# Routing of a product-key expert layer: key numbers on bf16, the slot as the inner index, the best scores copied by ScalarE

## The chip, the cores and the metric

The kernel runs on one core of a Trainium2 chip. The metric is the time of one execution on the device in microseconds, the median over runs. A second source is the profile: one execution as the hardware profiler recorded it, with every instruction of every engine.

The engines are TensorE (PE, its weight loads PEld), VectorE (DVE), ScalarE (ACT), GpSimd (POOL) and SyncE (SP, which here only issues DMAs). Each works through its own queue in program order.

## The reference

The network has two mLSTM blocks with their feed-forward layers and one block with attention, which ends in an expert layer (PEER) and a final norm, on 256 tokens of width 1024. The change lies in the expert layer:

```python
def block(xb):                                              # 128 tokens
    q = (xb @ w_q).reshape(n, PEER_HEADS, 2, PEER_HALF)     # 8 heads, 2 halves
    s = jnp.einsum('nhpc,hpkc->nhpk', q, sub_keys)          # 128 keys per half
    s_top, i_top = lax.top_k(s, PEER_TOPK)                  # the best 16 of each half
    cand_s = (s_top[:, :, 0, :, None] + s_top[:, :, 1, None, :]).reshape(n, PEER_HEADS, -1)
    cand_i = (i_top[:, :, 0, :, None] * N_KEYS + i_top[:, :, 1, None, :]).reshape(n, PEER_HEADS, -1)
    best_s, best_pos = lax.top_k(cand_s, PEER_TOPK)         # the best 16 of 256 pairs
    ids = jnp.take_along_axis(cand_i, best_pos, axis=-1)
    gate = jax.nn.softmax(best_s, axis=-1)
    act = gelu(jnp.einsum('nd,nhkd->nhk', xb, u[ids]))
    return jnp.einsum('nhk,nhkd->nd', (gate * act), v[ids])
```

## The kernel before, in words

The kernel doesn't gather experts. It computes the hidden value of all 16384 experts for all 256 tokens (128 "units" of 128 experts each, weights `pu`), multiplies them by a dense weight that is zero for experts not chosen, and multiplies by `pv`. The dense weights come out of the routing by one-hot products on TensorE.

Every weight tile streams through one helper: a DMA brings `wraw`, ScalarE rounds it to `whi` (L113), and the remainder `wlo` (L119) is a subtract on the engine `ws.sub`. In the stretch of interest `ws.sub` is GpSimd; `weights()` sets it to VectorE when it begins. Four tiles of `whi` and three of `wlo` are held, so a new one starts when a unit of TensorE is finished. A unit is 24 matmuls (L279 to L281), whose result ScalarE passes through Gelu into `store` (L228). Two banks hold results, so unit j + 2 needs the Gelu of unit j.

The last stretch has this order in the program. First sixteen query units with their key scores. Then a loop over the first 72 of the 128 units (`STORE`). After each unit the loop calls `bg(UBUD)` with `UBUD` 2.6, which hands background work to the queues: it adds 2.6 to a credit, and while the credit is above zero it draws one step from the first generator in the list and takes the number that the step yields off the credit. So the yields of a generator decide behind which unit each of its steps stands in the queues of all engines. The list holds the last `keys` generators (top 16 of the scores), then `route(0)`, `route(1)` and `weights()`.

`route(t)`, for 128 tokens, is nearly all VectorE: the key numbers as float (`fi`, L1627), the 256 sums of each head (`cand`, L1631), eight steps of top 16 (L1612 to L1616, values into `best`, places into `pos`), place to pair of slots by a mask and a shift (L1639, L1640), cast to `pf` (L1642), the best score `top` of each head (L1644), subtract (L1645), exponential on ScalarE (which needs a table load in front and another behind it, for the Gelu), sum, reciprocal, multiply. Then for both halves: compare the slot with 0 to 15 (`eq`, L1655), multiply by the key numbers (L1659), and add over the sixteen slots (L1662), which gives the key number of each chosen place. Three transposes on TensorE (L1667: gates, first ids, second ids) and VectorE's copies from PSUM (L1669 to L1674) close the route.

`weights()` begins with two `onehots` (L1686, L1688) and for four tokens at a time issues 12 one-hot products (L1712), whose result ScalarE copies into `stg` (L1715) on its way to DRAM. Later, `weighted(j)` reads it back (`wt`).

Of the kernel before, what the change touches and what calls it, by code (L numbers as in the profile page):

```python
# [8 lines left out]
F32 = mybir.dt.float32  # L9
F32R = mybir.dt.float32r  # L10
U32 = mybir.dt.uint32
BF16 = mybir.dt.bfloat16
AF = mybir.ActivationFunctionType
OP = mybir.AluOpType
PSUM = bass.MemoryType.PSUM

P = 128
T = 256
# [116 lines left out]
def build(ctx: ExitStack, tc: tile.TileContext, A, out):  # L135
    nc = tc.nc
# [37 lines left out]
    sc = nc.scalar  # L174
    ve = nc.vector
# [5 lines left out]
    def col(name, l=None, i=0, n=1):  # L181
        o, w = COLS[(name, l)] if l is not None else COLS[name]
        t, o = (cols[0], o) if o < EARLY else (cols[1], o - EARLY)
        return t[:, o + i:o + i + n]
# [40 lines left out]
    def actv(o, i, func, **kw):  # L225
        if func in tables and table[0] not in tables[func]:
            tab(tables[func][0])
        sc.activation(o, i, func, **kw)  # L228
# [95 lines left out]
    def modulated(src, r, scale, shift, between=None):  # L324

        hi, lo = big("h_h", dt=F32R), big("h_l", dt=F32R)
        ts = []
        for k in range(KC + 1):
            if k < KC:
                t = small("ta", bufs=3)  # L330
                ve.scalar_tensor_tensor(out=t, in0=src[:, k, :], scalar=scale[:, k:k + 1], in1=r, op0=OP.mult,
                                        op1=OP.mult)
                ts.append(t)
            flush()
            if k == 0 and between:
                between()
            if k == 0 and between or k == KC and not between:
                continue
            k -= 1 if between else 0
            t = ts[k]  # L340
            if shift is None:
                split_chunk(t, hi[:, k, :], lo[:, k, :])
            else:
                b = shift[:, k:k + 1]
                actv(hi[:, k, :], t, AF.Identity, bias=b)
                pending.append(lambda k=k, t=t, b=b: ve.scalar_tensor_tensor(
                    out=lo[:, k, :], in0=t, scalar=b, in1=hi[:, k, :].bitcast(F32), op0=OP.add, op1=OP.subtract))
            if k in PK:
                ws.pump()
        return pairs(hi, lo)  # L350

    def premod(l, g, isc):
        s = b1.tile([P, KC], F32, name="premod", tag="premod", bufs=2)
        ve.scalar_tensor_tensor(out=s, in0=mods[l][:, isc * 8:isc * 8 + 8], scalar=1.0, in1=col(g, l, n=8),
                                op0=OP.add, op1=OP.mult)
        return s
# [767 lines left out]
    h = modulated(x, r, premod(0, "g_pre_mix", 1), mods[0][:, 0:8], between)  # L1124
    h = modulated_rows(layer(0, h), premod(1, "g_pre_mix", 1), mods[1][:, 0:8])
    fill(1)
    h = modulated_rows(layer(1, h), col("g_mix_2", n=8), None)
# [464 lines left out]
    pp = ctx.enter_context(tc.tile_pool(name="pp", bufs=1))  # L1592
# [3 lines left out]
    ghl = [[pp.tile([P, T], F32R, name="gl", tag="gl", bufs=2)]]  # L1596
    pp.tile([P, 32], F32, name="padh")
    ghl[0].insert(0, pp.tile([P, T], F32R, name="gh", tag="gh", bufs=2))
    iota = pp.tile([P, 16], F32, name="iota")
    nc.gpsimd.iota(iota, pattern=[[1, 16]], base=0, channel_multiplier=0, allow_small_or_imprecise_dtypes=True)  # L1600

    iotn = pp.tile([P, P, NB], BF16, name="iotn")
    nc.gpsimd.iota(iotn, pattern=[[1, P], [0, NB]], base=0, channel_multiplier=0, allow_small_or_imprecise_dtypes=True)
# [19 lines left out]

    def route(t):
        X = mybir.AxisListType.X
        fi = pp.tile([P, 16, 16], F32, name="fi", tag="fi", bufs=1)
        ve.tensor_copy(fi, iu[:, t])  # L1627
        cand = pp.tile([P, 8, 16, 16], F32, name="cand", tag="st8", bufs=2)
        s2 = sv[:, t].rearrange("p (h s) k -> p h s k", s=2)
        f2 = fi.rearrange("p (h s) k -> p h s k", s=2)  # L1630
        ve.tensor_tensor(out=cand, in0=s2[:, :, 0, :, None].to_broadcast([P, 8, 16, 16]),  # L1631
                         in1=s2[:, :, 1, None, :].to_broadcast([P, 8, 16, 16]), op=OP.add)
        best = pp.tile([P, 8, 16], F32, name="best", tag="best", bufs=1)
        pos = pp.tile([P, 2, 8, 16], U32, name="pos", tag="pos", bufs=1)
        yield 2.7
        for hd in range(8):
            top16(cand[:, hd].rearrange("p a b -> p (a b)"), best[:, hd, :], pos[:, 0, hd, :])
            yield 2.4
        ve.tensor_scalar(pos[:, 1], pos[:, 0], 15, None, op0=OP.bitwise_and)  # L1639
        ve.tensor_scalar(pos[:, 0], pos[:, 0], 4, None, op0=OP.logical_shift_right)  # L1640
        pf = pp.tile([P, 2, 8, 16], F32, name="pf", tag="pf", bufs=1)
        ve.tensor_copy(pf, pos)  # L1642
        top = pp.tile([P, 8], F32, name="top", tag="top", bufs=1)
        ve.tensor_copy(top, best[:, :, 0])  # L1644
        ve.tensor_tensor(out=best, in0=best, in1=top[:, :, None].to_broadcast([P, 8, 16]), op=OP.subtract)  # L1645
        actv(best, best, AF.Exp)
        sm8 = pp.tile([P, 8], F32, name="sm8", tag="sm8", bufs=1)
        ve.tensor_reduce(sm8, best, axis=X, op=OP.add)
        ve.reciprocal(sm8, sm8)
        ve.tensor_tensor(out=best, in0=best, in1=sm8[:, :, None].to_broadcast([P, 8, 16]), op=OP.mult)  # L1650
        yield 2.0
        dst = [best.rearrange("p h k -> p (h k)")]
        for s in range(2):
            eq = pp.tile([P, 8, 16, 16], F32, name="eq", tag="st8", bufs=2)
            ve.tensor_tensor(out=eq.rearrange("p h k a -> p (h k) a"),  # L1655
                             in0=pf[:, s].rearrange("p h k -> p (h k)")[:, :, None].to_broadcast([P, P, 16]),
                             in1=iota[:, None, 0:16].to_broadcast([P, P, 16]), op=OP.is_equal)
            yield 2.4
            ve.tensor_tensor(out=eq, in0=eq, in1=f2[:, :, s, None, :].to_broadcast([P, 8, 16, 16]), op=OP.mult)  # L1659
            yield 2.4  # L1660
            ids = pf[:, s].rearrange("p h k -> p (h k)")
            ve.tensor_reduce(ids, eq.rearrange("p h k a -> p (h k) a"), axis=X, op=OP.add)  # L1662
            dst.append(ids)
            yield 2.4
        tr = aux_bank()
        for n, d in enumerate(dst):
            nc.tensor.transpose(tr[:, n * P:(n + 1) * P], d, ident)  # L1667
        ts = slice(t * P, (t + 1) * P)
        ve.tensor_copy(ijc[:, :, ts], tr[:, P:3 * P].rearrange("p (s t) -> p s t", s=2))  # L1669
        g = small("tb", bufs=3)[:, 0:P]  # L1670
        ve.tensor_copy(gpt[:, 0, ts], tr[:, 0:P])
        ve.tensor_tensor(out=g, in0=tr[:, 0:P], in1=gpt[:, 0, ts], op=OP.subtract)
        ve.tensor_copy(gpt[:, 1, ts], g)
        ve.tensor_tensor(out=gpt[:, 2, ts], in0=g, in1=gpt[:, 1, ts], op=OP.subtract)  # L1674
        yield 1.5
# [49 lines left out]
    for grp in range(4):  # L1725
# [3 lines left out]
        for i in range(4):  # L1729
# [3 lines left out]
            if hp == 0:  # L1733
# [3 lines left out]
                h = pairs(hh, hl)  # L1737
# [251 lines left out]
```

## Time and profile before

| | us |
|---|---|
| median of 3 runs | 2106.22 |
| lowest and highest run | 2101.06, 2108.39 |
| the profiled execution | 2108.57 |
| its span, first to last instruction | 2106.8 |
| TensorE busy in the span | 2026.7 |
| VectorE busy | 1386.8 |
| ScalarE busy | 1115.0 |
| GpSimd busy | 234.2 |

The profiled execution is one run among others; its time is its span and what the device needs around it. The mean granted clock of TensorE in it is 0.988 of full speed (2.4 GHz; the lower level is 1.2 GHz). A timeline row gives the start, the duration, engine, line, operation, result and inputs; in brackets stands how long the engine sat idle before it and what ended that.

### The profile page before, as it was taken

To read this page: it belongs to the slowest core of one execution; us is meant where nothing else is said; L and a number is where in the kernel's file an instruction comes from. 1 tells how busy PE (TensorE), PEld (TensorE's weight loads), DVE (VectorE), ACT (ScalarE), POOL (GpSimd) and SP (SyncE) were. 2 spreads that over 40 slices of the span, in tenths; PEclk is the share of its full clock that TensorE was granted. 3 is DMA by queue.
4 is the path that set the end of the run, shared out by engine and by line. 5 is a ranking of instruction groups with operands and counts; after the bars stand their busy time and mean duration, and the time that the engine had idled before them with its cause. 6 is when DMAs were issued, how large, how long until landed. Compare 5 with 4: busy or idle time off the path is not lost.

```text
span 2106.8 us, 37569 instructions
## 1 busy us (share of the span) xinstructions
PE 2026.7 (96%) x14926; PEld 1796.3 (85%) x14926; DVE 1386.8 (66%) x2278; ACT 1115.0 (53%) x1971; POOL 234.2 (11%) x185
## 2 busy tenths in 40 slices
PE   5989999999999899989999999889999999999998
PEld 3986678888976899879888999889999899998887
DVE  2765566656865665456677689887775555557776
ACT  3473565555746656564566544444444444445444
POOL 0101100000011000000100068840000000000000
PEclk9999999999999999999999999999999999999999
DMA  8863867874643665564333545445557766667774
GB/s 339 292 200 69 324 251 249 313 261 143 202 110 119 211 212 187 161 228 155 127 118 115 187 164 177 159 146 190 191 180 241 230 215 210 215 210 244 235 229 151
DMA packets 150044, 419.10 MB, mean 199 GB/s; under 512 B 15483, under 2 KB 56748, under 8 KB 147180
## 3 DMA queue, kind: packets, MB, share of 16 engines
q1 hardware_dynamic: 135676, 354.22, 51.7%
q0 software_dynamic: 11344, 43.61, 5.8%
q10 hardware_dynamic: 2848, 18.88, 2.2%
q8 instruction: 117, 1.92, 0.4%
q14 instruction: 59, 0.48, 0.1%
HBM read 397.02 MB, written 19.64 MB: 198 GB/s over the span
## 4 chain that ended last, share of the span: by engine, by line
PE 86%; DVE 5%; DMA 4%; ACT 3%; issue 1%; SPq 0%; POOL 0%; ACTq 0%; DVEq 0%
PE mm L279 13%; PE mm L280 13%; PE mm L281 13%; PE acc L394 9%; PE acc L395 9%; PE acc L396 9%; PE aux L1712 4%; PE aux L728 2%; DMA wraw<-wA 2%; ACT whi L113 1%; DVE eq L1659 1%; DMA wraw<-wB 1%; PE acc L1498 1%; PE acc L279 1%; PE acc L280 1%
## 5 line engine op out<-in xcount | busy, mean ns | idle before, releaser
L119 DVE TENSOR_TENSOR wlo<-wraw,whi 128x1024 fp32r<-128x1024 f32 x540 | 658.6, 1225 | 350.6 <-PE acc L395 129.0
L113 ACT CAST whi<-wraw 128x1024 fp32r<-128x1024 f32 x593 | 621.8, 1049 | 350.8 <-PE acc L396 197.2
L279 PE MATMUL mm<-h_h,whi 128*128 128x256 f32 x2440 | 690.1, 283 | 7.2 <-ACT sz L228 7.1
L280 PE MATMUL mm<-h_l,whi 128*128 128x256 f32 x2440 | 683.8, 280 | 1.7 <-DVE h_l L239 1.7
L281 PE MATMUL mm<-h_h,wlo 128*128 128x256 f32 x2440 | 680.2, 279 | 4.0 <-DVE wlo L119 2.3
L279 PEld LDWEIGHTS mm<-h_h,whi 128*128 128x128 f32 x2440 | 462.8, 190 | 16.5 <-ACT sz L228 7.2
L280 PEld LDWEIGHTS mm<-h_l,whi 128*128 128x128 f32 x2440 | 461.9, 189 | 4.8 <-DVE h_l L239 1.9
L281 PEld LDWEIGHTS mm<-h_h,wlo 128*128 128x128 f32 x2440 | 461.5, 189 | 5.1 <-DVE wlo L119 2.7
L395 PE MATMUL acc<-wlo,gh 128*128 128x512 f32 x512 | 202.6, 396 | 0.0
L394 PE MATMUL acc<-whi,gh 128*128 128x512 f32 x512 | 201.2, 393 | 0.0
L396 PE MATMUL acc<-whi,gl 128*128 128x512 f32 x512 | 200.7, 392 | 0.0
L228 ACT ACTIVATE store<-mm 128x256 f32<-128x256 f32 x128 | 49.3, 385 | 194.8 <-PE mm L281 194.6
L119 POOL TENSOR_TENSOR wlo<-wraw,whi 128x1024 fp32r<-128x1024 f32 x53 | 144.6, 2739 | 35.0 <-PE mm L281 25.0
L396 PEld LDWEIGHTS acc<-whi,gl 128*128 128x128 f32 x512 | 96.1, 188 | 22.2
L394 PEld LDWEIGHTS acc<-whi,gh 128*128 128x128 f32 x512 | 96.2, 188 | 20.7
L395 PEld LDWEIGHTS acc<-wlo,gh 128*128 128x128 f32 x512 | 96.0, 188 | 19.0
L396 PE MATMUL acc<-whi,f_l 128*128 128x512 f32 x256 | 101.1, 395 | 0.0
L394 PE MATMUL acc<-whi,f_h 128*128 128x512 f32 x256 | 100.8, 394 | 0.0
L395 PE MATMUL acc<-wlo,f_h 128*128 128x512 f32 x256 | 100.0, 391 | 0.0
L1712 PE MATMUL aux<-obg,oab 128*128 128x128 bf16 x768 | 96.0, 297 | 3.9 <-DVE obg L1688 3.9
L1712 PEld LDWEIGHTS <-oab 128*128 128x128 bf16 x768 | 85.4, 117 | 6.5 <-DVE obg L1688 4.1
L239 DVE TENSOR_TENSOR gl<-ta,gh 128x256 fp32r<-128x256 f32 x128 | 54.6, 426 | 51.9 <-ACT gh L238 51.9
(432 smaller groups left out, 2917.2 us busy)
## 6 DMA issues: line engine op xcount, KB each, us to landing
wraw<-wA SPq DMA_DIRECT2D x236, 512.0 KB, 3.9
wraw<-pu SPq DMA_DIRECT2D x128, 512.0 KB, 3.3
wraw<-pv SPq DMA_DIRECT2D x128, 512.0 KB, 3.6
wraw<-wB SPq DMA_DIRECT2D x101, 512.0 KB, 3.3
wada<-w_ada POOLq DMA_DIRECT2D x38, 1024.0 KB, 9.5
wd<-stg ACTq DMA_DIRECT2D x16, 1024.0 KB, 4.0
wt<-wd SPq DMA_DIRECT2D x16, 1024.0 KB, 7.3
wada<-w_ada SPq DMA_DIRECT2D x8, 1024.0 KB, 12.2
```

Source lines behind the costliest of these rows:

```text
L113: nc.scalar.copy(self.hi[i], self.raw[i])
L119: self.sub.tensor_tensor(out=self.lo[i], in0=self.raw.pop(i), in1=self.hi[i].bitcast(F32), op=OP.subtract)
L228: sc.activation(o, i, func, **kw)
L239: pending.append(lambda: ve.tensor_tensor(out=lo, in0=src, in1=hi.bitcast(F32), op=OP.subtract))
L279: mm(o, hi, xh, start=start, stop=False)
L280: mm(o, hi, xl, start=False, stop=False)
L281: mm(o, lo, xh, start=False, stop=stop)
L394: mm(o, xh, wh, start=start, stop=False)
L395: mm(o, xh, wl, start=False, stop=False)
L396: mm(o, xl, wh, start=False, stop=stop)
L728: mm(o[32 * g:32 * g + 32, 0:T], t[:, g * 8 + k, :], r[:, g, 4 * k:4 * k + T], start=k == 0, stop=k == 7, tile_position=(0, 32 * g))
L1712: mm(o[:, i * P:(i + 1) * P], eq[:, 0, :, i], ob[:, n, :, i], start=n == 0, stop=n == 2)
```

## The change

The iota becomes a bf16 tile of 16 x 16 with the slot number constant along the last index. `fi` and `pf` become bf16; all their values are whole numbers up to 127, which bf16 holds exactly. In `eq` the order of the indices is turned: head, slot `a`, chosen place `k`, with `k` innermost, where it was head, `k`, `a`. So the compare reads `pf` along `k` and the iota as it lies; the multiply reads one key number for sixteen neighbours; the reduce adds over `a`, which is no longer the innermost index in memory. `eq` occupies the same buffer as before, half used. The sums go to a tile `ids` of its own (f32, in a buffer of tag `tk`), no longer back into `pf`. The compare yields 1.8 where it yielded 2.4. `top` is copied by ScalarE.

```diff
-    iota = pp.tile([P, 16], F32, name="iota")
-    nc.gpsimd.iota(iota, pattern=[[1, 16]], base=0, channel_multiplier=0, allow_small_or_imprecise_dtypes=True)
+
+    iota = pp.tile([P, 16, 16], BF16, name="iota")
+    nc.gpsimd.iota(iota, pattern=[[1, 16], [0, 16]], base=0, channel_multiplier=0, allow_small_or_imprecise_dtypes=True)
...
-        fi = pp.tile([P, 16, 16], F32, name="fi", tag="fi", bufs=1)
+        fi = pp.tile([P, 16, 16], BF16, name="fi", tag="fi", bufs=1)
...
-        pf = pp.tile([P, 2, 8, 16], F32, name="pf", tag="pf", bufs=1)
+        pf = pp.tile([P, 2, 8, 16], BF16, name="pf", tag="pf", bufs=1)
         ve.tensor_copy(pf, pos)
         top = pp.tile([P, 8], F32, name="top", tag="top", bufs=1)
-        ve.tensor_copy(top, best[:, :, 0])
+        sc.copy(top, best[:, :, 0])
...
         dst = [best.rearrange("p h k -> p (h k)")]
+        ids = pp.tile([P, T], F32, name="ids", tag="tk", bufs=2).rearrange("p (s h k) -> p s h k", s=2, h=8)
         for s in range(2):
-            eq = pp.tile([P, 8, 16, 16], F32, name="eq", tag="st8", bufs=2)
-            ve.tensor_tensor(out=eq.rearrange("p h k a -> p (h k) a"),
-                             in0=pf[:, s].rearrange("p h k -> p (h k)")[:, :, None].to_broadcast([P, P, 16]),
-                             in1=iota[:, None, 0:16].to_broadcast([P, P, 16]), op=OP.is_equal)
+
+            eq = pp.tile([P, 4096], BF16, name="eq", tag="st8", bufs=2)[:, 0:2048].rearrange("p (h a k) -> p h a k", h=8, a=16)
+            ve.tensor_tensor(out=eq, in0=pf[:, s, :, None, :].to_broadcast([P, 8, 16, 16]),
+                             in1=iota[:, None].to_broadcast([P, 8, 16, 16]), op=OP.is_equal)
+            yield 1.8
+            ve.tensor_tensor(out=eq, in0=eq, in1=f2[:, :, s, :, None].to_broadcast([P, 8, 16, 16]), op=OP.mult)
             yield 2.4
-            ve.tensor_tensor(out=eq, in0=eq, in1=f2[:, :, s, None, :].to_broadcast([P, 8, 16, 16]), op=OP.mult)
-            yield 2.4
-            ids = pf[:, s].rearrange("p h k -> p (h k)")
-            ve.tensor_reduce(ids, eq.rearrange("p h k a -> p (h k) a"), axis=X, op=OP.add)
-            dst.append(ids)
+            ve.tensor_reduce(ids[:, s], eq.rearrange("p h a k -> p h k a"), axis=X, op=OP.add)
+            dst.append(ids[:, s].rearrange("p h k -> p (h k)"))
             yield 2.4
```

## Rows read from the trace of the kernel before

**Rows 1.** The page's first part: busy time, share of the span, instructions per engine.
```profile
PE 2026.7 (96%) x14926; PEld 1796.3 (85%) x14926; DVE 1386.8 (66%) x2278; ACT 1115.0 (53%) x1971; POOL 234.2 (11%) x185
```

**Rows 2.** Timeline of TensorE, both routes: start, duration, instruction, idle time before it.
```profile
1343.49 0.47 PE L1667 MATMUL aux<-ident,pf 128*128 128x128 f32 x1 [5.50 <-DVE pf L1662]
...
1393.40 0.33 PE L1667 MATMUL aux<-ident,pf 128*128 128x128 f32 x1 [1.47 <-DVE pf L1662]
1397.61 1.58 PE L1712 MATMUL aux<-obg,oab 128*128 128x128 bf16 x12 [3.88 <-DVE obg L1688]
```

**Rows 3.** Windows: PE, PEld, DVE, ACT, POOL busy, then granted clock, DMA.
```profile
1343.40:1347.80 4.40, 4.31 (x20) 4.31 (x21) 3.73 (x8) 0.00 (x0) 2.24 (x1) 0.50 0.61 183
...
1420.00:1440.00 20.00, 20.00 (x172) 19.65 (x172) 14.85 (x18) 8.52 (x14) 0.00 (x0) 1.00 0.58 211
```

**Rows 4.** Timeline of VectorE, first route.
```profile
1315.09 2.39 DVE L1645 TENSOR_TENSOR best<-best,top 128x128 f32<-128x128 f32 x1
...
1323.24 2.29 DVE L1655 TENSOR_TENSOR eq<-pf,iota 128x2048 f32<-128x2048 f32 x1
1325.57 4.38 DVE L1659 TENSOR_TENSOR eq<-eq,fi 128x2048 f32<-128x2048 f32 x1
1329.98 2.29 DVE L1662 TENSOR_REDUCE pf<-eq 128x128 f32<-128x2048 f32 x1
1332.19 4.54 DVE L1655 TENSOR_TENSOR eq<-pf,iota 128x2048 f32<-128x2048 f32 x1
1336.77 4.34 DVE L1659 TENSOR_TENSOR eq<-eq,fi 128x2048 f32<-128x2048 f32 x1
1341.15 2.29 DVE L1662 TENSOR_REDUCE pf<-eq 128x128 f32<-128x2048 f32 x1
```

**Rows 5.** Timeline of GpSimd in the same stretch.
```profile
1314.93 2.40 POOL L119 TENSOR_TENSOR wlo<-wraw,whi 128x1024 fp32r<-128x1024 f32 x1 [0.37 <-PE mm L281]
...
1320.63 2.40 POOL L119 TENSOR_TENSOR wlo<-wraw,whi 128x1024 fp32r<-128x1024 f32 x1 [0.45 <-PE mm L281]
1323.51 22.13 POOL L119 TENSOR_TENSOR wlo<-wraw,whi 128x1024 fp32r<-128x1024 f32 x6 [0.48 <-ACT whi L113]
```

**Rows 6.** The line of the multiply, both routes: shortest, median, longest in ns.
```profile
L1659 DVE TENSOR_TENSOR eq<-eq,fi x4: 4345/4371/4386, 1325.6 to 1386.7; 128x2048 f32<-128x2048 f32 x4
```

**Rows 7.** Timeline of ScalarE around the exponential of the first route.
```profile
1320.44 0.39 ACT L228 ACTIVATE store<-mm 128x256 f32<-128x256 f32 x1 [1.53 <-PE mm L281]
...
1322.13 0.31 ACT L228 ACTIVATE best<-best 128x128 f32<-128x128 f32 x1
1322.35 1.03 ACT L113 CAST whi<-wraw 128x1024 fp32r<-128x1024 f32 x1
...
1324.69 0.39 ACT L228 ACTIVATE store<-mm 128x256 f32<-128x256 f32 x1
```

**Rows 8.** Groups by line and shape, VectorE: count, busy us, mean ns, idle before.
```profile
L1688 DVE TENSOR_TENSOR obg<-oab,gpt 128x1536 bf16<-128x1536 bf16 x64 | 61.3, 958 | 2.2
L1686 DVE TENSOR_TENSOR oab<-iotn,ijc 128x1024 bf16<-128x1024 bf16 x64 | 44.1, 688 | 39.5 <-PE aux L1712 39.5
```

**Rows 9.** The same view: instructions that read with a step, and a cast.
```profile
L1175 DVE TENSOR_TENSOR blk<-tok,pe 128x480 f32<-128x480 f32 x4 | 3.8, 989 | 9.4 <-ACT tok L1172 9.4
...
L1627 DVE CAST fi<-iu 128x256 f32<-128x256 uint32 x2 | 0.6, 280 | 0.0
...
L1243 DVE COPY tcm<-tz 128x120 f32<-128x120 f32 x2 | 0.5, 270 | 0.0
...
L1244 DVE COPY tcm<-tz 128x56 f32<-128x56 f32 x2 | 0.4, 209 | 0.0
```

**Rows 10.** Timeline of GpSimd at the start of the expert layer.
```profile
1214.74 1.18 POOL L1603 IOTA iotn<- 128x512 bf16 x1
1219.16 2.41 POOL L119 TENSOR_TENSOR wlo<-wraw,whi 128x1024 fp32r<-128x1024 f32 x1 [3.24 <-issue]
```

**Rows 11.** Timeline of VectorE behind the second route's transposes.
```profile
1394.75 0.88 DVE L1673 CAST gpt<-tb 128x128 bf16<-128x128 f32 x1
```

## The prediction

> **What bounds the kernel now.** I read the page first: TensorE is busy 96% of the span, VectorE 66% [rows 1]. So a change on VectorE's routing can only act where TensorE waits for it. The list of TensorE's instructions in the routing stage shows three such places, each marked by an idle time in brackets [rows 2]: the third transpose of the first route came 5.50 us late, that of the second route 1.47 us late (both held by the last `tensor_reduce`, L1662), and the first one-hot product 3.88 us late. After that TensorE is full: 20.00 of 20.00 us in the stretch 1420 to 1440 [rows 3]; the end moves one for one with the moment at which the second route's transposes are released and with the TensorE work still left then. Behind the first wait the granted clock is 0.50, the lower of the two levels, for 4.4 us [rows 3].
>
> The chain behind that wait is VectorE's alone, and its rows show why it is long [rows 4]. Per route there are two halves of compare (L1655), multiply (L1659) and reduce (L1662). The first compare takes 2.29 us, the second 4.54; each multiply takes 4.38 or 4.34. The excess is a wait for GpSimd, which makes `wlo` (L119) in this stretch: L1645 is a small subtract, yet it runs from 1315.09 to 1317.48, and GpSimd's subtract runs from 1314.93 to 1317.33 [rows 4, 5]. An instruction of VectorE with two SBUF inputs waits until GpSimd's is done, and GpSimd then waits for VectorE: six `wlo` subtracts take 22.13 us instead of 6 x 2.40 [rows 5]. The reduce has one input and runs beside GpSimd (2.29 us). All four multiplies of both routes lie between 4345 and 4386 ns, so the second route repeats the first [rows 6].
>
> **Part by part: the queue order.** The generator's costs decide where TensorE meets the transposes. When a route's first step is drawn in unit j=6, 2.2 of credit are left; each later unit adds 2.6. The first transposes come behind costs of 2.7 + 8 x 2.4 + 2.0 + 6 x 2.4 = 38.3 before and 37.1 after (two yields of 1.8 for 2.4): 2.2 + 2.6 n exceeds both first at n = 14, so both stand behind unit 20. The second route's stand behind 78.1 before (n = 30, unit 36) and 75.7 after (n = 29, unit 35). So TensorE's queue meets them one unit earlier. Since VectorE releases them, that is no gain: unit 36, which lay in front of the wait, now lies behind it. One unit is 2.85 us by the distance of GpSimd's subtracts, 5.70 us for two [rows 5]; I take 2.8. Cost: **+2.8 us**. ScalarE's queue position of the exponentials (behind units 14 and 29) stays.
>
> **The copy of the best scores on ScalarE.** On VectorE it hid in the wait for the exponential. On ScalarE it stands behind that unit's Gelu, which waits for TensorE. Call the Gelu's start G: 1320.44, 0.39 us long; the exponential started at G + 1.69, gated by a table load [rows 7]. GpSimd's next subtract starts at G + 0.19 and holds until G + 2.59 [rows 5]. Now the copy ends at about G + 0.6 to 0.7 (under the 0.31 us of the 128-column exponential), L1645 starts then, finds GpSimd at work and ends 0.15 us behind it as in [rows 4, 5], at G + 2.74; the exponential starts at G + 2.78. That is **+1.09 us** on the chain of each route. Bounds: +0.2 if GpSimd were idle (only the copy is in front of the table load), +1.1 as worked out. I take the upper end, since GpSimd's subtract follows every unit's end at the same distance. Behind the waiting exponential ScalarE holds `whi` and the next Gelu (1322.35 and 1324.69 in [rows 7]); both come 1.1 us later. GpSimd's first subtract waits for that `whi` and shifts along, so the first compare still gets in ahead of it. TensorE may wait some tenths for a bank; the transposes' own wait covers that.
>
> **The compare** becomes bf16 with adjacent inner elements in all operands. The same form costs 688 ns for 1024 and 958 ns for 1536 elements [rows 8], so 0.527 ns each and 148 ns fixed: 1.23 us for 2048, against 2.29. Twice per route, on the chain: **-2.12 us**. Upper bound of its cost: 2.29, the f32 row.
>
> **The multiply** keeps 2.29 us of its own plus its wait. Its second input is now one element repeated sixteen times in the inner loop; the fast rows have neighbours there in every operand. Bounds 1.23 and 2.29; I take 2.29, the row of the same operation. The Trainium skill ("Vector Engine (DVE) Microarchitecture Reference", section 5.1) reports single speed for a two-source instruction with 2-byte operands when one input is a single element read 16 times; no row here shows that, and the other reading has its chance below.
>
> **The reduce** now reads with a stride: its inner index `a` lies 16 bf16 elements apart. Two places of the trace read with a step [rows 9]. L1175 (f32, step 16) takes 989 ns for 480 elements; at the compare's f32 pace of 1.04 ns and 148 ns fixed it would be 649, so the step costs 0.71 ns per element. L1243 and L1244 (copies with step -16) give (270 - 209) / 64 = 0.95 ns each; with the 156 ns that this leaves as fixed part, the contiguous cast L1627 has 0.48, so the step doubles the pace. The reduce is then 2.29 + 2048 x 0.71 = 3.7 us by the first, 0.15 + 2 x 2.13 = 4.4 by the second, and 2.29 if a reduce doesn't feel it. I take 3.7: an instruction at one element per step, as the reduce is. The first reduce of a route hides: between the multiply's end (1329.95) and the second compare's real start (1334.45) lie two subtracts of GpSimd, 4.5 us, whatever the reduce takes below that. The second one lies bare: **+1.4 us** per route.
>
> The Trainium skill (same page, section 5.2) gives 1.73 ns per column where one source jumps at every element, and L1175 agrees with 1.75; it also gives 2.50 for steps of 24 words, by which the reduce would be an estimated 5.3 us.
>
> **The rest.** The wider iota (256 elements) runs once; 512 elements take 1.18 us and GpSimd is idle 3.24 us behind [rows 10]: nothing. Without that idle time it would be some 0.5 us. In front of the first one-hot the cast L1673 took 0.88 us, held by the last of the six `wlo` subtracts [rows 11]; with the transposes one unit earlier, GpSimd has one subtract less and is done by then: 0.28 as the cast of L1627 [rows 9], **-0.6 us**, once.
>
> **Sum.** Per route 1.09 - 2.12 + 1.41 = +0.4; twice, with 2.8 and -0.6: **+3.0 us**. The profiled execution took 2108.57 us (span 2106.8), so 2111.6; it lies 2.35 above the median of the runs, 2106.22, from which I forecast **2109.2**. What is late next is the same: the transposes, with waits of about 5.9 us in the first route and 5.5 in the second; the clock's drop behind each is taken as unchanged.
>
> **Rivals.**
> - The reduce doesn't feel the stride. For it: no strided reduce in the trace; against: both strided rows. Per route 1.09 - 2.12, the rest as above: +0.2, 2106.4.
> - Slower: the reduce passes 4.5 us. From there GpSimd gets a third subtract in ahead of the second compare (some 2.2 us), on top of a bare second reduce. At 4.6: 1.09 - 2.12 + 2.2 + 2.31 = 3.5 per route, +9.2, 2115.4 (+0.44%). For it: the upper strided row is already at 4.4; against: L1175.
> - The multiply doubles its pace too: -2.12 more per route, -1.2 in all, 2105.0. For it: all types are 16 bits wide; against: the repeated element.
> - VectorE's bf16 instructions don't wait for GpSimd. No row has them side by side. The chain would be 1.23 + 2.29 + 3.7, twice, 14.4 instead of 20.1 us: -4.6 per route with the later exponential, -7.0, 2099.3.
> - The change doesn't do what it says: the compare stays at 2.29 us. +7.2, 2113.4.
>
> **How the numbers follow.** Forecast 0.50, reduce unchanged 0.17, reduce over 4.5 us 0.17, fast multiply 0.10, no wait for GpSimd 0.03, slow compare 0.03. The runs before spread from 2101.06 to 2108.39 us, so a median may be off by 2 or 3. The range 2103 to 2116 takes in the forecast with both prices of the reduce (up to 2110.6), the first three rivals and that spread. About 0.3% (6.3 us) is what a measurement of this kernel can tell from no change. Faster by more than that needs the free port or luck: 0.06. Slower: the long reduce, the slow compare, and part of the forecast's own spread: 0.23. Within: 0.71.
>
> **What the next profile would show.** L1655's successor at 1.23 us twice per route, plus a wait of 2.2 in the second half; the multiply at 4.4 with its wait; the reduce at 3.7; L1645 near 2.1 us, beginning after a copy on ScalarE; the exponential 2.8 us after its unit's Gelu; the second transposes behind unit 35, with a wait of 5 to 6 us. The prediction is wrong if GpSimd and VectorE meet in another order than before, if the lower clock lasts longer behind the longer second wait, or if the moved addresses of later tiles change TensorE's pace.

## The result and the profile after

| | before | after |
|---|---|---|
| median, us | 2106.0 | 2115.77 |
| lowest and highest run | 2101.06, 2108.61 | 2108.01, 2122.92 |
| the profiled execution | 2108.57 | 2119.49 |
| its span | 2106.8 | 2117.7 |

The ratio is 1.0051, with a 95% interval from 1.0037 to 1.0066: some 10.7 us slower. The forecast was 2109.2, +3.0, too little for a measurement to tell from no change; the time is at the upper edge of the range, and the loss is clear of the noise.

The line numbers after are one to three higher than before. The first part of the page, to be laid beside [rows 1]:

```profile
PE 2034.7 (96%) x14926; PEld 1804.2 (85%) x14926; DVE 1386.4 (65%) x2277; ACT 1114.9 (53%) x1973; POOL 227.7 (11%) x184
```

VectorE is busy for as long as before (1386.8). TensorE is busy 8.0 us longer (2026.7 before) with the same 14926 instructions. Something has become slower on the one engine that the change doesn't touch.

VectorE in the first route, the timeline of after (compare with [rows 4]):

```profile
1321.31 2.23 DVE L1646 TENSOR_TENSOR best<-best,top 128x128 f32<-128x128 f32 x1 [5.97 <-ACT top L1645]
...
1324.68 1.22 DVE L1658 TENSOR_TENSOR eq<-pf,iota 128x2048 bf16<-128x2048 bf16 x1
1325.93 4.38 DVE L1661 TENSOR_TENSOR eq<-eq,fi 128x2048 bf16<-128x2048 bf16 x1
1330.34 4.38 DVE L1663 TENSOR_REDUCE ids<-eq 128x128 f32<-128x2048 bf16 x1
1334.65 1.41 DVE L1658 TENSOR_TENSOR eq<-pf,iota 128x2048 bf16<-128x2048 bf16 x1
1336.09 4.38 DVE L1661 TENSOR_TENSOR eq<-eq,fi 128x2048 bf16<-128x2048 bf16 x1
1340.50 3.88 DVE L1663 TENSOR_REDUCE ids<-eq 128x128 f32<-128x2048 bf16 x1
```

Most rows are within 0.2 us of the prediction. The first reduce took 4.38 instead of 3.7, and the second compare 1.41 instead of 1.23 plus the wait of 2.2 that the last paragraph of the prediction names. Together they end where its sum has them: 4.5 us for what hides the reduce and 1.23 behind it, 5.73, against 4.38 + 1.41 = 5.79. ScalarE around the exponential (compare with [rows 7]):

```profile
1320.80 0.39 ACT L228 ACTIVATE store<-mm 128x256 f32<-128x256 f32 x1 [1.53 <-PE mm L281]
1321.08 0.20 ACT L1645 COPY top<-best 128x8 f32<-128x8 f32 x1
1321.30 1.28 ACT L218 ACT_TABLE_LOAD   x1
1323.57 0.31 ACT L228 ACTIVATE best<-best 128x128 f32<-128x128 f32 x1 [0.99 <-DVE best L1646]
```

The exponential starts 2.77 us behind its unit's Gelu (predicted 2.78, before 1.69). TensorE's waits from 1290 to 1640, by line (compare with [rows 2]):

```profile
PE aux L1668 <- DVE ids L1663: 11.9, 2, 6.0
PE aux L1713 <- DVE obg L1689: 3.2, 1, 3.2
```

Both waits of the transposes are near 6 us, as forecast (5.9 and 5.5), and nothing waits for `wlo` any more. So the routing does what the prediction says. Where, then, is the rest? Each unit leaves one Gelu on ScalarE, and the distance between the Gelus of two units is TensorE's time for what lies between. Timeline of ScalarE before, units 73 and 127 of the 128, which lie in the last stage (one unit and the twelve products with `pv` in turn):

```profile
1599.85 0.39 ACT L228 ACTIVATE store<-mm 128x256 f32<-128x256 f32 x1 [1.63 <-PE mm L281]
...
1897.57 0.39 ACT L228 ACTIVATE store<-mm 128x256 f32<-128x256 f32 x1 [1.63 <-PE mm L281]
```

The same two units after:

```profile
1604.95 0.39 ACT L228 ACTIVATE store<-mm 128x256 f32<-128x256 f32 x1 [1.75 <-PE mm L281]
...
1908.43 0.39 ACT L228 ACTIVATE store<-mm 128x256 f32<-128x256 f32 x1 [1.74 <-PE mm L281]
```

54 units take 297.72 us before and 303.48 after: 5.513 and 5.620 each, +5.76 in all, far behind the routing. The 256-column matmuls of the units carry it. TensorE's timeline before, first and nineteenth of nineteen in a row, and after, the same:

```profile
1801.26 0.28 PE L279 MATMUL mm<-h_h,whi 128*128 128x256 f32 x1
...
1803.30 0.28 PE L279 MATMUL mm<-h_h,whi 128*128 128x256 f32 x1
```

```profile
1804.58 0.28 PE L279 MATMUL mm<-h_h,whi 128*128 128x256 f32 x1
...
1806.72 0.28 PE L279 MATMUL mm<-h_h,whi 128*128 128x256 f32 x1
```

2.04 us for 18 distances before, 2.14 after: a matmul every 0.113 us, or every 0.119 on average, with no wait named and the granted clock 1.00 in both stretches. At full clock nearly every unit of this part of the program, before and after, shows one of these two paces; I call them the fast and the slow one.

What an execution needs up to the Gelu of unit 0 (1280.49 before) differs from one to the next by -4.5 to +6.3 us, whatever the kernel. So the stages are compared by the Gelus, counted from that of unit 0. After against before, so counted: +0.25 at unit 21 (first route done), +1.32 at 29, +4.51 at 69 (second route and one-hot products done), +4.73 at 73, +10.49 at 127. The stages that the prediction worked out gave 4.7 for its 3.0; the last stage, which it left out of its sum, gave 5.8.

### The profile page after: what moved, and what is told of

Its sections match the earlier page's. It is cut to its first block, busy times and chain, and to the rows that moved or that the text cites. A ratio compares the mean times of both kernels' runs of the same rounds, so it can differ in the third digit from the quotient of the medians.

```text
span 2117.7 us, 37571 instructions
## 1 busy us (share of the span) xinstructions
PE 2034.7 (96%) x14926; PEld 1804.2 (85%) x14926; DVE 1386.4 (65%) x2277; ACT 1114.9 (53%) x1973; POOL 227.7 (11%) x184
## 4 chain that ended last, share of the span: by engine, by line
PE 87%; DVE 6%; ACT 3%; DMA 3%; issue 1%; SPq 0%; POOL 0%; ACTq 0%; DVEq 0%
PE mm L279 13%; PE mm L280 13%; PE mm L281 13%; PE acc L394 10%; PE acc L396 9%; PE acc L395 9%; PE aux L1713 4%; PE aux L728 2%; ACT whi L113 1%; DVE eq L1661 1%; DMA wraw<-wB 1%; PE acc L279 1%; PE acc L1498 1%; DVE ids L1663 1%; PE acc L280 1%
## 5 line engine op out<-in xcount | busy, mean ns | idle before, releaser
L119 POOL TENSOR_TENSOR wlo<-wraw,whi 128x1024 fp32r<-128x1024 f32 x52 | 138.1, 2666 | 39.0 <-PE mm L281 27.0
```

Source lines behind the costliest of these rows:

```text
L119: self.sub.tensor_tensor(out=self.lo[i], in0=self.raw.pop(i), in1=self.hi[i].bitcast(F32), op=OP.subtract)
```

## The experiments

"Counted from unit 0" has the meaning above; "the last stage" is units 73 to 127.

**before_again** is the kernel before once more. It tells how far a profile repeats.

> The kernel before once more, for a second profile. In the two profiles at hand the last stage (units 73 to 127, one unit and twelve accumulating products each) goes at 5.51 us per unit before and 5.62 after, 5.8 of the 10.9 us between them. Theory A, addresses: the changed tiles lie 64 bytes lower and TensorE's pace hangs on that; this run shows 5.51 again. Theory B, a state: TensorE's 256-column matmuls go at 0.1135 or 0.119 us, the state is set by how TensorE was last halted and kept; this run may show 5.51 or 5.62, and the routing stage repeats (waits 5.5, 1.5, 3.9 us) within 0.3 us.

Counted from unit 0: +0.49 at unit 21, +0.85 at unit 73, +0.85 at unit 127; 5.51 per unit in the last stage. So the same kernel repeats to about 1 us by stage, and the last stage's pace came out the same in a second execution. The kernels below that keep the routing of before and only move tiles or alter the last stage spread further: from +0.74 to +2.13 at unit 73. A difference of 1 or 2 us up to there is thus not yet an effect of the edit. Most kernels have one profile each; in the ten that were timed over repeated runs (the changed kernel among them) the value at unit 127 lies inside the interval of the timed ratio.

**after_addr** is the changed kernel with all later tiles at their old addresses.

```diff
-    iota = pp.tile([P, 16, 16], BF16, name="iota")
+    pp.tile([P, 16], F32, name="padi")
+    pq = ctx.enter_context(tc.tile_pool(name="pq", bufs=1))
+    iota = pq.tile([P, 16, 16], BF16, name="iota")
...
-        fi = pp.tile([P, 16, 16], BF16, name="fi", tag="fi", bufs=1)
+        fi = pp.tile([P, 512], BF16, name="fi", tag="fi", bufs=1)[:, 0:256].rearrange("p (a b) -> p a b", a=16)
```

(`pf` is padded as `fi` is; the pool `pq` lies behind all others.)

> The changed kernel with every later tile at the address it had before (iota put behind the pool, fi and pf padded). Theory A (addresses): the last stage returns to 5.51 us per unit, total near +5 us over before (ratio 1.0024). Theory B (a state of TensorE, not the addresses): 5.61 to 5.62 may remain, total as measured for the change, +8 to +11 (ratio 1.004 to 1.005). The routing stage as in the changed kernel in both: waits of 6.0 us at both transposes.

Ratio 1.0026 [1.0010, 1.0041]; counted from unit 0, +4.03 at unit 73 and +4.03 at 127. ScalarE's timeline, units 73 and 127:

```profile
1599.86 0.38 ACT L228 ACTIVATE store<-mm 128x256 f32<-128x256 f32 x1 [1.63 <-PE mm L281]
...
1897.58 0.38 ACT L228 ACTIVATE store<-mm 128x256 f32<-128x256 f32 x1 [1.63 <-PE mm L281]
```

The last stage is back at 5.51, 297.72 us for the 54 units. About half of the loss has to do with where tiles lie, not with the routing's work.

**before_yield** makes the queue change alone: the compare's yield 1.8 in the kernel before.

```diff
-            yield 2.4
+            yield 1.8
```

> The kernel before with the compare's yield at 1.8 instead of 2.4, nothing else. Queue theory: the second transposes stand behind unit 35 instead of 36, VectorE's chain is as long as before, so their wait grows from 1.5 to about 4.3 us, the cast in front of the one-hots is 0.6 us shorter, and the kernel takes +2.2 us (ratio 1.001). Rival: the position costs nothing, since the chain releases the transposes at the same time: 0.

Ratio 1.0018 [1.0005, 1.0031]; +3.23 at unit 73. Of this, 1.07 arises in units 21 to 29, where TensorE ran at the slow pace; that leaves 2.2. The second transposes (TensorE's timeline) wait 5.24 us instead of the 1.47 of [rows 2]:

```profile
1390.50 0.48 PE L1667 MATMUL aux<-ident,pf 128*128 128x128 f32 x1 [5.24 <-DVE pf L1662]
```

They come just as long behind the Gelu of unit 29 as before (23.03 us in both). So VectorE releases them, and the step of the queue order is confirmed: a smaller yield made the kernel slower.

**bf16_only** has the opposite parts: bf16 and the index order, with `top` on VectorE, the yield 2.4, and the changed kernel's own addresses.

```diff
-        sc.copy(top, best[:, :, 0])
+        ve.tensor_copy(top, best[:, :, 0])
...
-            yield 1.8
+            yield 2.4
```

> The changed kernel with the copy of the best scores back on VectorE and the yield back at 2.4: bf16 and the turned index order alone. Chain theory: per route the two compares save 2.1 us, the bare second reduce costs 1.6 (3.9 instead of 2.3), the first reduce hides behind GpSimd: -0.5 per route, -1.0 us in all (ratio 0.9995). Rival: the strided reduces decide and the kernel is slower than before by 2 us or more.

Up to the last stage it is even with before: -0.38 at unit 29, +0.19 at 73 (-0.83 at 37, near what was expected). Then 5.62 per unit: +5.95 at unit 127, ratio 1.0034 [1.0021, 1.0047].

**addr_dve** is after_addr with `top` back on VectorE.

```diff
-        sc.copy(top, best[:, :, 0])
+        ve.tensor_copy(top, best[:, :, 0])
```

> The changed kernel at the old addresses (as after_addr) with the copy of the best scores back on VectorE; the yield of 1.8 stays. Chain theory: the exponential starts 1.7 us after its unit's Gelu instead of 2.8, each route is 1.1 us shorter, so unit 69 comes 1.9 us later than before (counted from unit 0) instead of 4.0. Rival (the wait for GpSimd would come anyway, at the sum): 4.0 stays.

+2.32 at unit 73 and at 127, ratio 1.0010 [0.9993, 1.0027]. The copy therefore costs 4.03 - 2.32 = 1.71 us for both routes, but some 1.06 of it is the slow pace of units 21 to 29, which after_addr had and this one not; 0.7 lies in front of unit 21, and the second route adds nothing. Counted from unit 0, the second transposes come at 115.0 us in after_addr and at 112.2 here, yet the granted clock is back at 1.00 at some 122.4 in both: the earlier ones have the longer stretch at the lower level, 1.2 GHz, behind them. Windows from the first of these transposes to nearly the end of that stretch, after_addr and then addr_dve (granted clock third from the right):

```profile
1391.50:1398.70 7.20, 3.98 (x23) 3.68 (x24) 6.49 (x12) 1.53 (x2) 0.00 (x0) 0.50 0.14 48
```

```profile
1397.10:1406.90 9.80, 6.58 (x35) 6.29 (x36) 7.24 (x12) 1.53 (x2) 0.00 (x0) 0.50 0.27 91
```

**before_low64** is the kernel before with the buffers of tag `st8` (`cand`, `eq`, `stg`, `wt`) and everything above them 64 bytes lower; `fi` goes to a pool behind, and nothing else changes.

```diff
-        fi = pp.tile([P, 16, 16], F32, name="fi", tag="fi", bufs=1)
+        if t == 0:
+            pp.tile([P, 240], F32, name="padf")
+        fi = pq.tile([P, 16, 16], F32, name="fi", tag="fi", bufs=1)
```

> The kernel before with only the buffers of tag st8 (cand, eq, stg, wt) and what lies above them 64 bytes lower (fi moved out of the pool, 960 bytes in its place). Address theory: the routing stage is as before (waits of 5.5, 1.5 and 3.9 us, each within 0.3), the last stage goes at 5.62 us per unit instead of 5.51, and the kernel is 6 to 7 us slower (ratio 1.003). Rival (TensorE's pace comes from the order of the routing stage or by chance): the last stage stays at 5.51, ratio 1.000.

+1.69 at unit 73, then 5.62 per unit: +7.45 at unit 127. Two rows of ScalarE's timeline, units 73 and 127:

```profile
1605.77 0.38 ACT L228 ACTIVATE store<-mm 128x256 f32<-128x256 f32 x1 [1.75 <-PE mm L281]
...
1909.25 0.39 ACT L228 ACTIVATE store<-mm 128x256 f32<-128x256 f32 x1 [1.75 <-PE mm L281]
```

303.48 us, to the hundredth what the changed kernel needs. The timed ratio, 1.0020 [0.9999, 1.0040], has room for this and for less.

**after_st8** is the changed kernel with 64 bytes in front of those buffers.

```diff
+        if t == 0:
+            pp.tile([P, 16], F32, name="pads")
```

> The changed kernel with 64 bytes of padding in front of the st8 buffers, so that wt and stg lie where they lay before, while the one-hot tiles stay 512 bytes lower. If wt's address decides: the last stage at 5.51 us per unit, and the span about 6 us under the changed kernel's from the first unit on. If the one-hot tiles decide: 5.62.

+3.67 at unit 73 and +3.67 at unit 127; 5.51 per unit. One pad of 64 bytes undoes the loss of the last stage. The one-hot tiles moved up by the same 64 (from 576 bytes below their old place to 512), so this doesn't tell which tile matters.

**before_low128** moves the same tiles of before by 128 bytes instead of 64, **before_low32** by 32 (`padf` of 224 or 248 instead of 240).

> The kernel before with the cand/eq/stg/wt buffers and all above them 128 bytes lower (before_low64: 64 bytes lower, units of 5.62 us in the last stage against 5.51). Theory (the place of these buffers within 128 bytes decides): 5.51 us per unit, ratio 1.000 within 0.0015. Rival (any lower address, or the distance to the tiles below them, decides): 5.62 per unit, +5.8 us from unit 73 to the end.

> The kernel before with the cand/eq/stg/wt buffers and all above them 32 bytes lower. If the place within 128 bytes decides in steps of 64: one of 5.51 or 5.62 us per unit through the last stage. If the two paces come from how a 64-byte row of wt lies across a border: something between (5.56), or 5.62.

128 bytes: 5.51 per unit, +2.13 at units 73 and 127, ratio 1.0014 [1.0001, 1.0028]. 32 bytes: 5.62, +1.06 at unit 73, +6.81 at 127. There is nothing in between.

**low64_noread** and **low64_noload** take away from before_low64 what the last stage does with `wt`: VectorE reads `sv` instead, or only the first two blocks are loaded.

```diff
-        w = wts[j // 8][:, :, j % 8, :]
+        w = sv[:, 0]
```

```diff
-            load_w(j // 8 + 1)
+            if j == 0:
+                load_w(1)
+            else:
+                wts[j // 8 + 1] = wts[j // 8 - 1]
```

> before_low64 with VectorE's weighted product of the last stage reading the fixed tile sv instead of wt (wt is still loaded; its values are left out of the output). If VectorE's reading of wt at the 64-byte lower place is what slows TensorE: 5.51 us per unit in the last stage. If it is the transfers into wt, or the state in which the stage is entered: 5.62 as in before_low64.

> before_low64 with wt loaded only twice (blocks 0 and 1) and reused afterwards; VectorE reads wt as before, the later blocks' weights are left out. If the transfers into wt slow TensorE: 5.62 us per unit up to about unit 80 and 5.51 after it. If VectorE's reading, or the state in which the stage is entered, decides: 5.62 all the way.

5.62 per unit in both, from unit 73 to 127. Neither use of `wt` alone makes this stage slow, and low64_kick below goes fast with both; the theory of a conflict with `wt` falls.

**low64_st8only** and **onehot_low64** split the tiles that had always moved together: only the `st8` buffers and the small tiles above them lower (a pad in front of `oab`), or only `oab` and `obg` (`top` and `sm8` moved into a pool behind).

> before_low64 with a 64-byte pad in front of the one-hot tiles oab and obg: these stand where they stood before, the cand/eq/stg/wt buffers 64 bytes lower. In every kernel so far the two moved together within 128 bytes. If the place of the cand/eq/stg/wt buffers decides: 5.62 us per unit in the last stage. If the place of the one-hot tiles, which TensorE reads, decides: 5.51.

> The kernel before with two small tiles (top, sm8) moved behind all others, so that only oab and obg stand 64 bytes lower. If the place of the one-hot tiles decides: 5.62 us per unit. If that of the cand/eq/stg/wt buffers does: 5.51.

Both 5.51; +0.74 and +1.21 at unit 73 and the same at 127. Neither group alone brings the slow pace, only both together. So no single tile's address "decides"; that was my own expectation, and it falls too. The first of the two is the weaker test: its routing took another course (the first transposes waited 1.38 us, not 5.5), so it came to the last stage on another way.

**low64_kick** disturbs TensorE three times in the slow last stage of before_low64.

```diff
+            if j == 12:
+                mm(aux_bank()[:, 0:P], x[:, 0, half[0]], ident, start=True, stop=True)
+            if j in (24, 36):
+                kick = small("tb", bufs=3)
+                sc.copy(kick, x[:, 0, :])
+                mm(aux_bank()[:, 0:P], kick[:, half[j // 36]], ident, start=True, stop=True)
```

> before_low64 with three disturbances of TensorE in the last stage: one extra 128-column matmul behind unit 84, and behind units 96 and 108 one that waits for a fresh copy of ScalarE (results unused). If the pace is a state that the stage was entered in and keeps: it changes from 5.62 to 5.51 us per unit at one or more of the three, and stays changed. If something within every unit sets it: 5.62 on both sides of all three, apart from the disturbed units themselves.

ScalarE's timeline: units 83 to 87 around the extra matmul, then 108 to 111 around the third disturbance.

```profile
1655.46 0.39 ACT L228 ACTIVATE store<-mm 128x256 f32<-128x256 f32 x1 [1.75 <-PE mm L281]
1661.08 0.38 ACT L228 ACTIVATE store<-mm 128x256 f32<-128x256 f32 x1 [1.75 <-PE mm L281]
1666.81 0.39 ACT L228 ACTIVATE store<-mm 128x256 f32<-128x256 f32 x1 [1.63 <-PE mm L281]
1672.33 0.39 ACT L228 ACTIVATE store<-mm 128x256 f32<-128x256 f32 x1 [1.63 <-PE mm L281]
1677.84 0.38 ACT L228 ACTIVATE store<-mm 128x256 f32<-128x256 f32 x1 [1.63 <-PE mm L281]
...
1794.87 0.38 ACT L228 ACTIVATE store<-mm 128x256 f32<-128x256 f32 x1 [1.63 <-PE mm L281]
1801.76 0.38 ACT L228 ACTIVATE store<-mm 128x256 f32<-128x256 f32 x1 [1.75 <-PE mm L281]
1807.39 0.39 ACT L228 ACTIVATE store<-mm 128x256 f32<-128x256 f32 x1 [1.76 <-PE mm L281]
1813.01 0.39 ACT L228 ACTIVATE store<-mm 128x256 f32<-128x256 f32 x1 [1.75 <-PE mm L281]
```

The distance is 5.62 up to unit 84, 5.73 in the unit with the extra matmul, and from then on 5.52 and 5.51 in every unit up to 108, across the second disturbance (6.77 once, then 5.51). The third turns it back: 6.89, then 5.63 and 5.62 to the end. Same tiles, same addresses, same work: the pace is a state that is kept from unit to unit, and one 128-column matmul or a short halt can turn it, or not. The addresses only bear on the state in which the stage is entered.

The starts of the matmuls in the traces, to the ns, show that this state comes from the stage in front. At the slow pace every sixth distance is 0.124 or 0.125 us and the others 0.117 to 0.119; at the fast one all are 0.113 or 0.114. In unit 71, the last in front of the last stage, 14 of the 20 profiles run slowly. In seven of them the last long distance ends at the unit's last matmul, and all seven come out fast; in the other seven it ends three matmuls earlier, and these are the seven kernels that stay slow. The six that are fast in unit 71 stay fast. What shifts that pattern by three matmuls isn't shown. The chip doesn't decide it: on three of the chips used, kernels of both paces ran.

**after_nogps** is after_addr with `wlo` made by VectorE during the routes, so that VectorE's instructions run with GpSimd idle.

```diff
     def route(t):
         X = mybir.AxisListType.X
+        ws.sub = nc.vector
```

> The changed kernel at before's addresses, with wlo made by VectorE instead of GpSimd from the first route on: VectorE's routing instructions then run with GpSimd idle. Not meant to be fast (1.22 us more per unit on VectorE). Theory (a strided bf16 reduce is slowed beside GpSimd's subtracts, and both its durations of 4.4 and 3.9 us contain that): compare 1.22, multiply 2.29, reduce 3.2 to 3.6 us four times. Rival (a one-source reduce doesn't feel GpSimd and 3.9 is its own time): reduce 3.85 to 3.95.

Groups by line: count, busy us, mean ns of one.

```profile
L1666 DVE TENSOR_REDUCE ids<-eq 128x128 f32<-128x2048 bf16 x4 | 15.8, 3944 | 0.0
L1664 DVE TENSOR_TENSOR eq<-eq,fi 128x2048 bf16<-128x2048 bf16 x4 | 9.2, 2288 | 0.0
L1661 DVE TENSOR_TENSOR eq<-pf,iota 128x2048 bf16<-128x2048 bf16 x4 | 4.9, 1220 | 0.0
```

Compare 1.22 and multiply 2.29 are their own times, without GpSimd's. The reduce takes 3.94 (3.82 to 4.02): my theory that GpSimd lengthens it falls for the 3.88 of the second reduce; why the first one of a route takes 4.1 to 4.4 beside two subtracts stays open (it hides). The kernel as a whole is slow, 2119.44 us, since VectorE now makes TensorE wait 8.7 us for `wlo`.

**best** asks whether the waits of the transposes can be put away: addr_dve with larger yields, so that the transposes stand behind units 22 and 40, when their operands are ready, and the one-hot blocks follow more densely.

```diff
-            yield 1.8
+            yield 3.1
...
-        yield 1.5
+        yield 4.1
...
-    WCOST = 1.3
+    WCOST = 1.08
```

(All three yields of the halves are 3.1.)

> bf16 and the turned order at the old addresses, the copy on VectorE, and the yields raised (3.1 for the six steps of each route, 4.1 for the transposes, 1.08 for a block of weights), so that the transposes stand behind units 22 and 40, the second exponential behind 32, the first one-hot product behind 41, and the last block behind 68 as before. Queue theory: TensorE works through units where it waited; the waits of 5.5, 1.5 and 3.9 us shrink to under 1.5 each, the lower clock behind them goes, and the kernel is 8 to 12 us faster than before (ratio 0.995). Rival: VectorE's chain is only met later and the waits come back at the end of the stage or in front of the last stage: ratio 0.999 to 1.001.

Ratio 0.9988 [0.9970, 1.0007], -2.66 at unit 73, where -8 to -12 was expected. -8.20 at unit 21 shows the first wait gone with its low clock. TensorE's waits:

```profile
PE aux L1715 <- DVE obg L1691: 6.5, 11, 2.8
PE mm L281 <- POOL wlo L119: 2.1, 2, 1.4
PE mm L279 <- ACT store L228: 1.3, 1, 1.3
```

The wait moved: one of 2.8 us at the first one-hot block, and ten of 0.36 where three blocks stand in one unit. VectorE has two buffers of `oab` and `obg`, so the third block is made only when TensorE has done the first. Such a third block added 1.95 us to its unit (a gap between unit matmuls of 4.83 us against 2.88), where half of the 2.67 for two blocks would be 1.34.

**best2** mends both: the first block two units behind the transposes, and each third `oab` in the dead tile `sv`.

```diff
-        yield 4.1
+        yield 4.1 if t == 0 else 6.0
...
-    WCOST = 1.08
+    WCOST = 1.04
...
-        eq = pp.tile([P, 2, P, NB], BF16, name="oab", tag="oab", bufs=2)
+        if b % 3 == 2:
+            eq = sv.rearrange("p a b c -> p (a b c)").bitcast(BF16).rearrange("p (a m n) -> p a m n", a=2, n=NB)
+        else:
+            eq = pp.tile([P, 2, P, NB], BF16, name="oab", tag="oab", bufs=2)
```

> The kernel best with two edits: the first one-hot block stands two units behind the second transposes instead of one, and every third block's compare writes into the dead sv tile, so that three blocks in a row find three buffers (WCOST 1.04: 2, 3, 2, 3 blocks per unit). Theory (what best gave back was lost at two places: 2.8 us of wait and some 2.3 us of low clock at the first one-hot, and some 0.36 us of wait in each of ten units with a third block): counted from unit 0, -9 to -12 us against before at unit 73, and the same at the end; median ratio about 0.995. Rival (VectorE's 1.65 us per block sets the pace of denser blocks whatever the buffers): the third blocks keep their waits, and unit 73 lies at -4 to -6.

2098.43 us, ratio 0.9959 [0.9941, 0.9977]: -9.36 at units 73 and 127, within the expectation. It is faster than both kernels. Waits:

```profile
PE aux L1718 <- DVE obg L1694: 2.3, 1, 2.3
PE mm L281 <- POOL wlo L119: 2.1, 2, 1.4
PE mm L279 <- ACT store L228: 1.3, 1, 1.3
```

The ten waits are gone (the third block's gap is 4.30); the one at the first block stays, 2.3.

**before_sched** gives the f32 kernel before the same queue places and third buffer.

> The kernel before, in f32 and with its old lines, with the queue places and the third buffer of best2. If the queue places alone are what helps and the bf16 form is worth nothing once the waits are gone: unit 73 within 1.5 us of best2's, ratio within 0.001 of it. If the shorter compares of the bf16 form are what lets the transposes come without a wait: some 1 to 3 us of wait at each transposes, and 3 to 8 us more than best2 with the clock's drop behind it.

2102.56 us, ratio 0.9977 [0.9963, 0.9991], -5.83 at unit 73: neither of the two expectations. The transposes wait for nothing here either, so the shorter compares are not what allows the new places. But more waits for GpSimd's `wlo` come up:

```profile
PE mm L281 <- POOL wlo L119: 5.7, 6, 1.4
PE aux L1715 <- DVE obg L1691: 2.3, 1, 2.3
PE mm L279 <- ACT store L228: 1.3, 1, 1.3
```

5.7 us against 2.1 in best2; the 3.6 between them answers to the 3.5 between the two kernels (9.36 - 5.83). So in these two profiles the bf16 form is worth 3.5 us once the queue is in order; the intervals of the two timed ratios overlap, so the size is not certain. By the waits it comes by way of GpSimd, whose 27 subtracts of this stretch take 82.1 us here (18 in 52.82 and 9 in 29.24) and 77.9 in best2 (17 in 48.27, one in 2.40 and 9 in 27.18): the shorter compares of VectorE seem to hold it up less, which no run tests by itself.

## Why the prediction was wrong

- **The step that failed: "The rest" in the sum.** It priced the wider iota and the cast and said nothing of the new places of the tiles, and the first paragraph took the TensorE work still left behind the routing as fixed. The places came up only in the last clause, "if the moved addresses of later tiles change TensorE's pace", with no price. The price is 54 units of 0.107 us, +5.76; with the old places, after_addr, it is gone. Why the new places lead to the slow pace stays open. It was to be had from the trace of before: units at both paces stand in its routing stage. Behind the 4.4 us of [rows 3] a unit took 2.72 us (the Gelus of units 21 and 29 start at 1348.61 and 1370.37, 21.76 for eight), ahead of it 2.85 [rows 5], with the same 24 matmuls at full clock. Why it changed I had not asked. The last stage of before ran at the fast pace (a matmul every 0.113 us), so with 56 units still to come there, the slow one was a rival of some 6 us upward.
- **The queue order, +2.8.** Right: before_yield shows 2.2 without the slow units and 3.23 with them. It includes the cast's -0.6, which comes with the earlier place, so the sum has 2.8 - 0.6 = 2.2 too.
- **ScalarE's copy, +1.09 per route.** The mechanism is right to 0.01 us (the exponential 2.77 behind the Gelu), and the first route's transposes come 1.08 us later in after_addr than in addr_dve. On what comes behind them it is too large: of the 1.71 for both routes 1.06 is the pace of units 21 to 29. The prediction took "the clock's drop behind each" as unchanged; the later transposes had a shorter one, which gave the rest back.
- **The compare, -2.12 per route.** Right: 1.22 us of its own. The wait of 2.2 named for the second one was 0.2. That figure didn't fit the sum, where 4.5 - 3.7 = 0.8 is left of it behind the longer reduce; as the reduce took another 0.7, nearly all of it was hidden.
- **The multiply, 2.29 plus its wait.** Right: 4.38, and 2.29 alone. The Trainium skill ("Vector Engine (DVE) Microarchitecture Reference", section 5.1) has single speed for a two-source instruction with 2-byte operands of which one is an element read 16 times, and the trace agrees.
- **The reduce, 3.7.** Slightly small: 3.88 bare, 3.94 alone. That is (3.94 - 0.15) / 2048 = 1.85 ns for an element, nearer to L1175's 1.75 than to the 2.1 from L1243 [rows 9]. The Trainium skill's 1.73 ns for one source that jumps by 4 KiB at every element (same page, section 5.2) is met nearly; its 2.50, which it gives for both sources or the result stepping by 24 words, is not reached. The rival above 4.5 us didn't come.
- **The cast, -0.6.** Right in kind: L1674 takes 0.23 instead of the 0.88 of [rows 11].
- **Sum of the routing stages.** +4.73 for +3.0; 1.07 of the difference is units 21 to 29 at the slow pace, the rest, 0.6, is within what the kernel before differs from itself (0.85) and from its copies with moved tiles (up to 2.13).
- **The chances.** "Slower" had 0.23, from the long reduce, the slow compare and the spread. It came for none of these reasons. That the measured 2115.77 still lies under the range's 2116 is luck: the range reached so far up for a reduce that didn't come.

## What to carry to other kernels

Where one engine is full for hundreds of microseconds, look whether the same instruction runs at two paces in the trace of before, and price both for all that is left; a change that only moves tiles can pick either. Before making the work in front of a wait cheaper, see whether the waiting instruction can simply stand later in its queue: here that, with a third buffer behind it, gave 5.8 us with the old arithmetic (before_sched), and the cheaper arithmetic alone, bf16_only without its last stage, gave nothing. And when a wait is moved, look for the next one: here the gain of the first attempt went into the buffers of the stage behind.

## What the runs showed that I had not expected

- TensorE went at one of two paces, 0.1135 and 0.119 us for a 256-column f32 matmul, at a granted clock of 1.00 and without any wait in the records. In the last stage it is kept over all 54 units; one extra 128-column matmul turned 5.62 us per unit into 5.51, one halt of 0.77 us did nothing, and another of the same length turned it back.
- Moving two groups of tiles by 32 or 64 bytes, or by that and whole multiples of 128, went with the slow pace in the last stage (after, bf16_only, before_low32, before_low64 and the three kernels made from it that move both groups), moving them by whole multiples of 128 or moving only one group with the fast one. How the one-hot stage leaves the matmuls in unit 71 goes with the outcome in all 20 profiles; why it leaves them so is not settled, and nothing was shown to conflict. Whether one extra matmul at the start of the last stage would give the changed kernel its 5.8 us back wasn't tried.
- An instruction of VectorE with two inputs in bf16 waits for GpSimd as one in f32 does (multiply 4.38 beside it, 2.29 without), while the second reduce of a route, which reads one input, takes 3.83 to 3.94 us beside it and 3.82 to 4.02 with GpSimd idle. In best and best2 the same reduce took 4.12 to 4.26 us; why isn't shown.
